# Layer 0 of a hybrid encoder trunk: k norms, low-rank products, logits and inverse roots written another way

## The chip, the cores and the metric

The kernel runs on one core of a Trainium2 chip. The time is that of the device, in microseconds, from the first to the last instruction of the program; lower is better. All arithmetic is in 32 bits. TensorE multiplies numbers of type fp32 in two instructions, and numbers of type fp32r in one; the kernel reaches the accuracy of fp32 with fp32r by splitting an operand into a high part (rounded to fp32r) and a low part (what the rounding left), and by adding the products high x high, high x low and low x high.

## What is computed

The reference has two layers over 1024 positions of width 1024. Layer 0 mixes positions with two groups of heads side by side, layer 1 with chunked attention; each layer then has a squared-ReLU MLP and a gated embedding. Only layer 0 and one helper are touched here. Its parts, cut to what the change names:

```python
# group A (RWKV-7, 8 heads of 64): decay and learning rate from a second low-rank product
w_log = -softplus(-(w0 + tanh(xw @ w1) @ w2)) - 0.5
a = sigmoid(a0 + (xa @ a1) @ a2)
...
# group B (gated DeltaNet, 4 heads of 128)
q = l2norm(heads(qkv[..., :B_WIDTH])) * (B_HEAD_DIM ** -0.5)
k = l2norm(heads(qkv[..., B_WIDTH:2 * B_WIDTH]))
beta = sigmoid(beta_logit)                                       # logits: h @ 8 columns of the input weight
g = -exp(a_log) * softplus(alpha_logit + dt_bias)
o = chunk_gated_delta_rule(q, k, v, beta, g)                     # k_dec = k * exp(gc_last - gc)
o = rmsnorm(o, norm_g) * silu(gate)
```

Here l2norm divides by the root of the sum of squares plus 1e-6, and rmsnorm by the root of the mean square plus 1e-6.

## The kernel before

Activations are kept transposed: 128 partitions hold 128 channels, the free axis holds positions. Layer 0 works on two halves of 512 positions. In each half there are eight units, alternately a pair of RWKV heads and one DeltaNet head: 16 units in all. A unit passes five stages: **in** (dense products of the input with 128 columns of weight at a time), **front** (everything before the triangular inverse), **mid** (the inverse), **back** (the recurrence over four chunks of 128) and **post** (output norm and gate).

Each stage is a generator, and `run` interleaves them as lanes: there is one lane each for in, mid, back and post, two for front, and one for the cumulative decays. A lane that yields a name sleeps for the time that the table `LAT` gives for it, on a clock that only matrix products advance; a lane that yields a tuple waits until another lane has marked it. So the order of the work is made when the program is written out: small products of a lane that is ready go between the dense products, which are last in line. A scheduler that simulates the engines then orders the instructions of each engine, and each engine works through its queue in that order.

The dense product (`dense_part`, `mm3`, all products by the helper `mm` at L180, transposes by `tr` at L195) takes three passes for each of 8 blocks of 128 input channels: high weight with the high and the low part of the input, low weight with the high part. Weights come by DMA on SyncE's queue into a ring `wraw` of two buffers, ScalarE casts the high part (L306), VectorE subtracts the low part (L307). Results are read from PSUM by VectorE.

PSUM in this layer: two banks `dense` for the dense products, two banks `tp` that the front lanes and the post lane share (tiles named `tp`, `st`, `sc`, `pp` in the profile), and single banks for mid and back (`iz`, `pm`, `ch`, `y`). Work tiles of 128x512 come from pools with a number of slots: 11 slots `f` for the fronts and the in lane (`L0_FRONT`), 14 slots `b` for what the fronts hand to back and post (`L0_BACK`). A tile waits until its slot is free.

What the change and the prediction touch:

- `rsqrt_small` (L285 to L294): 1 / sqrt(x) on VectorE for a few numbers per partition. A first guess by integer arithmetic on the bits (L289), then three Newton steps of three operations each (L292 to L294): ten operations, each on the result of the one before. It is called by `row_stats` (sums over all channels), `rwkv_post`, `gdn_front`, `gdn_post` and, in layer 1, `attn_in`.
- `lora`: the first low-rank product, at the start of each half. For decay and learning rate its result is `lwa`, 128x512, in fp32 (tile `lao`); the upper 64 rows get a tanh.
- `rwkv_front`: the second low-rank product, two fp32 products over 64 rows each, `wa2` with `lwa`, put next to each other by `together` (rows of the profile: `tp<-lao,wa`). After it come the tanh and the running sums that give the decay.
- `gdn_logits`: the 8 logit columns as a dense product. A zeroed tile of 128x1024 takes 8 columns of each 128; it is split and multiplied like every other weight, three passes for each of 8 blocks. `gdn_scalars` transposes the 8 rows of the result in 4 pieces and computes beta and the decay.
- `gdn_front`: after the convolutions of k and q (tile `KQ`) come the squares of both on ScalarE (L1081), sums over the 128 channels by one-column products with the squares as stationary operand (rows `st<-ones,f`, 8 fp32 products, 16 instructions), the inverse roots of all 8 columns, and from them `cs`, `ncs`, `hin` (for k) and `phi` (for q). Then the score products in two pairs (`sc<-KQ`), each into a bank `tp`, read with `ncs`. Then the start of the inverse, the convolution of v, and four transposes of k whose result ScalarE scales into `kd` (L1132).
- `gdn_post`: output norm. The sum of squares of the output comes by one-column products; VectorE squares `phi`, combines the two, takes the inverse root and multiplies by `phi` again (L1189 to L1193).
- `masks`: the constants `blk`, `blkr` and `cent`.

Of the kernel before, what the change touches and what calls it, by code (L numbers as in the profile page):

```python
# [8 lines left out]
F32 = mybir.dt.float32  # L9
# [8 lines left out]
P = 128  # L18
# [13 lines left out]
L0_FRONT = {"raw": 6, "f": 11}  # L32
# [80 lines left out]
class Trunk:  # L113
# [140 lines left out]
    def masks(self, cst):  # L254
# [19 lines left out]
        self.blk = cst.tile([P, P], F32, tag="blk", name="blk")  # L274
        nc.gpsimd.memset(self.blk, 0.0)
        nc.gpsimd.memset(self.blk[0:64, 0:64], 1.0)
        nc.gpsimd.memset(self.blk[64:128, 64:128], 1.0)
        self.blkr = cst.tile([P, P], F32R, tag="blkr", name="blkr")
        nc.vector.tensor_copy(self.blkr, self.blk)
        self.cent = cst.tile([P, P], F32, tag="cent", name="cent")  # L280
        nc.gpsimd.tensor_scalar(self.cent, self.blk, -1.0 / 64, None, op0=ALU.mult)
# [3 lines left out]
    def rsqrt_small(self, out, x, shape, tag):  # L285
# [3 lines left out]
        nc.vector.tensor_scalar(out.bitcast(I32), x.bitcast(I32), -0.5, 1597463007.0,  # L289
                                op0=ALU.mult, op1=ALU.add)  # L290
        for _ in range(3):
            nc.vector.tensor_tensor(w, out, out, op=ALU.mult)  # L292
            nc.vector.scalar_tensor_tensor(w, w, -0.5, x, op0=ALU.mult, op1=ALU.mult)
            nc.vector.scalar_tensor_tensor(out, w, 1.5, out, op0=ALU.add, op1=ALU.mult)  # L294
# [275 lines left out]
    def l0_in(self, units):  # L570
# [3 lines left out]
        for u, (nm, p, hf) in enumerate(units):  # L574
            if u % 8 == 0:
# [32 lines left out]
                if hf == 0:  # L608
# [6 lines left out]
                    self.wa2 = fr.tile([P, 512], F32, tag="wa2", name="wa2")  # L615
                    nc.sync.dma_start(out=self.wa2, in_=a["wa2"])
# [15 lines left out]
                sc["lwa"] = yield from self.lora(0, [(0, 64, 0), (64, 128, 1)], "la")  # L632
                nc.scalar.activation(sc["lwa"][0:64], sc["lwa"][0:64], AF.Tanh)
# [56 lines left out]
    def lora(self, i, mus, key, between=None):  # L690
# [16 lines left out]
        out = (self.l0 if key == "lg" else self.fr).tile([P, HB], F32, tag=key + "o", name=key + "o", bufs=2 if key == "lg" else 1)  # L707
# [8 lines left out]
    def gdn_logits(self):  # L716
        nc, a = self.nc, self.a
        raw = self.wp.tile([P, 1024], F32, tag="wraw", name="wraw")
        nc.gpsimd.memset(raw, 0.0)
        nc.sync.dma_start(out=raw.rearrange("p (k c) -> p k c", k=NK)[:, :, 0:8], in_=a["wba"])  # L720
        ba = self.t2()
        yield from self.dense_half(self.split_w(raw), lambda ps: nc.vector.tensor_tensor(ba[0:8, 0:HB], ps[0:8], self.rs[0:8],
                                                                                         op=ALU.mult))
        return ba
# [1461 lines left out]
```

## Time and profile before

| | us |
|---|---|
| median of 3 runs | 3078.52 |
| lowest and highest of them | 3070.69, 3079.13 |
| the profiled execution | 3086.63 |
| its span, first to last instruction of the cores' records | 3084.8 |
| TensorE busy in the span | 2970.1 (96%) |
| VectorE, ScalarE, GpSimd busy | 2209.9, 1486.2, 552.9 |

PE is TensorE's products, PEld its weight loads, DVE VectorE, ACT ScalarE, POOL GpSimd, SP SyncE. A row of the timeline gives the start, the length, the engine, the line, the operation, the tiles (out<-in) with their sizes, how many instructions were merged, and in brackets the idle time before them and what ended it. A row of a group gives the count, the busy time, the mean of one in ns, and the engine's idle time before the group. A wait is "who <- for whom: total us, times, longest". The granted clock is TensorE's, as a share of its full speed. Because products are pipelined, the length of a product is more than the time it holds the queue; that is read from one start to the next.

### The profile page before, as it was taken

The page shows a single profiled execution, that of the slowest core. Times are in us where ns is not written, and L with a number is a line of the kernel's source. Part 1 is how long each engine was busy: PE and PEld are TensorE (multiplying, and loading weights), DVE is VectorE, ACT ScalarE, POOL GpSimd, SP SyncE. Part 2 cuts the span into 40 slices and gives each one's busy share as a digit, 9 for nine tenths or more (in the row PEclk, how much of TensorE's full clock was granted, in tenths as well). Part 3 has the DMA queues.
Part 4 walks back from the last instruction along what each step waited for, and adds up shares of the span by engine and source line. Part 5 has one row for each costly group of instructions (what it writes and reads, how often), then busy time and mean ns, then how long its engine had stood idle before and what let it go on. Part 6 is the DMA issues. An engine that isn't in the chain of part 4 may idle for free.

```text
span 3084.8 us, 47290 instructions
## 1 busy us (share of the span) xinstructions
PE 2970.1 (96%) x17254; PEld 2457.1 (80%) x17254; DVE 2209.9 (72%) x4546; ACT 1486.2 (48%) x2957; POOL 552.9 (18%) x985
## 2 busy tenths in 40 slices
PE   8999999999999999999999999999999999999999
PEld 6777777777777888788887988898878888888887
DVE  7556766667758777788887676676768777788883
ACT  4333433434437555544444465565757555544441
POOL 5434442443500000000005111111210000000002
PEclk9899999999999999999999999999999999999999
DMA  4212112212346444754424211110256444654433
GB/s 145 64 55 62 54 49 75 61 55 68 110 157 227 162 150 151 262 166 151 151 95 131 70 44 40 43 61 23 75 181 223 163 154 153 237 190 150 150 103 116
DMA packets 194857, 368.49 MB, mean 119 GB/s; under 512 B 46800, under 2 KB 49088, under 8 KB 194624
## 3 DMA queue, kind: packets, MB, share of 16 engines
q1 hardware_dynamic: 163808, 309.35, 31.4%
q10 hardware_dynamic: 30816, 56.11, 4.7%
q8 instruction: 136, 2.23, 0.3%
q14 instruction: 97, 0.79, 0.1%
HBM read 268.86 MB, written 96.53 MB: 118 GB/s over the span
## 4 chain that ended last, share of the span: by engine, by line
PE 71%; DVE 14%; DMA 6%; ACT 4%; issue 2%; POOL 1%; SPq 0%; ACTq 0%; DVEq 0%; POOLq 0%
PE dps L180 57%; PE ch L180 2%; PE po L180 2%; DVE act L1283 2%; PE pm L180 1%; PE iz L180 1%; PE pt L195 1%; DMA late<-in_w 1%; PE sn L180 1%; PE tp L180 1%; DMA late<-hd 1%; DVE late L1431 1%; DMA wraw<-in_w_out 1%; PE py L180 1%; DVE wlo L307 1%
## 5 line engine op out<-in xcount | busy, mean ns | idle before, releaser
L180 PE MATMUL dps<-r,act 128*128 128x512 f32 x3720 | 872.9, 392 | 2.0 <-DVE xw L1550 0.8
L180 PEld LDWEIGHTS dps<-r,act 128*128 128x128 f32 x3720 | 698.0, 188 | 157.0 <-issue 1.2
L180 PE MATMUL dps<-xg,whi 128*128 128x512 f32 x1280 | 436.0, 421 | 11.2 <-ACT whi L306 7.4
L1647 POOL TENSOR_TENSOR pn<-pn,prs 128x512 f32<-128x512 f32 x32 | 47.3, 1483 | 1542.6 <-ACT prs L389 1419.5
L180 PE MATMUL dps<-wq,act 128*128 128x384 f32 x1536 | 307.8, 347 | 13.8 <-DVE vs L1909 6.0
L180 PEld LDWEIGHTS dps<-xg,whi 128*128 128x128 f32 x1280 | 236.2, 197 | 62.2 <-ACT whi L306 7.6
L180 PEld LDWEIGHTS dps<-wq,act 128*128 128x128 f32 x1536 | 269.6, 193 | 17.7 <-DVE vs L1909 7.6
L180 PE MATMUL dps<-xg,wlo 128*128 128x512 f32 x640 | 260.7, 407 | 2.6 <-DVE wlo L307 2.6
L1282 ACT CAST act<-act 128x512 fp32r<-128x512 f32 (+2 forms) x281 | 159.3, 600 | 142.0 <-PE dps L180 59.8
L1283 DVE TENSOR_TENSOR act<-act 128x512 fp32r<-128x512 f32 (+2 forms) x281 | 180.1, 669 | 4.6 <-ACT act L1282 4.6
L180 PE MATMUL dps<-act 128*128 128x512 f32 x720 | 176.5, 393 | 2.0 <-DVE late L1404 2.0
L1282 ACT CAST act<-late 128x512 fp32r<-128x512 f32 x210 | 123.7, 620 | 100.4 <-PE dps L180 73.8
L180 PE MATMUL dps<-late,act 128*128 128x512 f32 x672 | 166.6, 392 | 0.0
L180 PEld LDWEIGHTS dps<-act 128*128 128x128 f32 x720 | 136.2, 189 | 32.1 <-DVE late L1404 2.4
L1283 DVE TENSOR_TENSOR act<-late,act 128x512 fp32r<-128x512 f32 x210 | 139.1, 687 | 31.1 <-ACT act L1282 30.9
L180 PEld LDWEIGHTS dps<-xg,wlo 128*128 128x128 f32 x640 | 125.0, 195 | 32.5 <-DVE wlo L307 3.8
L180 PEld LDWEIGHTS dps<-late,act 128*128 128x128 f32 x672 | 126.0, 188 | 27.7
L180 PE MATMUL dps<-xw,act 128*128 128x512 f32 x576 | 145.9, 392 | 0.2 <-ACT act L1282 0.2
L1550 DVE TENSOR_TENSOR xw<-xw,dps 128x512 f32<-128x512 f32 x192 | 130.0, 682 | 17.3 <-PE dps L180 17.2
L306 ACT CAST whi<-wraw 128x1024 fp32r<-128x1024 f32 (+1 forms) x79 | 81.8, 1035 | 107.6 <-PE dps L180 77.1
L180 PEld LDWEIGHTS dps<-xw,act 128*128 128x128 f32 x576 | 107.9, 188 | 24.4 <-ACT act L1282 0.7
L180 PE MATMUL po<-ptile,vs 128*128 128x256 f32 (+1 forms) x576 | 106.8, 295 | 15.5 <-ACT ptile L352 9.7
(488 smaller groups left out, 5600.7 us busy)
## 6 DMA issues: line engine op xcount, KB each, us to landing
hb<-late ACTq DMA_DIRECT2D x196, 256.0 KB
act<-hb SPq DMA_DIRECT2D x158, 256.0 KB
late<-in_w SPq DMA_DIRECT2D x60, 512.0 KB
act<-in_w SPq DMA_DIRECT2D x112, 256.0 KB
wraw<-in_w_in SPq DMA_DIRECT2D x55, 512.0 KB
braw<-hb SPq DMA_DIRECT2D x80, 256.0 KB
wraw<-in_w_out SPq DMA_DIRECT2D x21, 512.0 KB
wraw<-in_w_qkv SPq DMA_DIRECT2D x21, 512.0 KB
```

What stands on the lines that cost most here:

```text
L180: return self.begin(self.nc.tensor.matmul(out, lhsT, rhs, start=start, stop=stop, skip_group_check=again))
L195: return self.begin(self.nc.tensor.transpose(out, in_, ident))
L306: nc.scalar.copy(hi, raw)
L307: nc.vector.tensor_tensor(lo, raw, hi.bitcast(F32), op=ALU.subtract)
L1282: A.copy(hi, s)
L1283: V.tensor_tensor(lo, s, hi.bitcast(F32), op=ALU.subtract)
L1431: V.tensor_tensor(t, u, v, op=ALU.subtract)
L1550: V.tensor_tensor(x[n][:, hs[hf]], x[n][:, hs[hf]], ps, op=ALU.add)
L1647: G.tensor_tensor(pn, pn, prs[:, sl], op=ALU.mult)
```

## The change

In words:

- `rsqrt_small` takes another first guess, one Newton step with tuned constants (three operations) and one step of higher order (four operations): eight in all.
- `wa2` and the first low-rank result `lwa` are split into high and low parts of type fp32r; each of the two second products becomes three fp32r passes instead of one fp32 product. `wa2` is loaded through the ring `wraw`. The unsplit `lwa` is now a work tile `f`.
- `gdn_logits` loads the 64 numbers per partition without a zeroed tile, puts the high and low parts of the 8 columns side by side as 16 columns, and takes two passes for each block (high and low part of the input). `gdn_scalars` transposes 16 rows, and one reduction adds the two halves.
- `gdn_front` makes the four transposes of k before the norms. ScalarE squares each transposed piece straight from PSUM and sums along the row in the same instruction, with the result tile `kd` as scratch; then it scales the pieces into `kd` from the same bank. The inverse root is taken for the 4 columns of k only. The squares of q and their four sums come later, the sums after the convolution of v; `phi` becomes a constant times the sum plus a constant.
- `gdn_post` needs one operation instead of three ahead of its root and none behind it, since q's norm only enters through the epsilon.
- `blk` becomes a view of `blkr`, and the work slots `f` go from 11 to 10.

The diff, cut:

```diff
-L0_FRONT = {"raw": 6, "f": 11}
+L0_FRONT = {"raw": 6, "f": 10}
...
     def rsqrt_small
-        nc.vector.tensor_scalar(out.bitcast(I32), x.bitcast(I32), -0.5, 1597463007.0,
+        nc.vector.tensor_scalar(out.bitcast(I32), x.bitcast(I32), -0.5, 1595932665.0,
                                 op0=ALU.mult, op1=ALU.add)
-        for _ in range(3):
-            nc.vector.tensor_tensor(w, out, out, op=ALU.mult)
-            nc.vector.scalar_tensor_tensor(w, w, -0.5, x, op0=ALU.mult, op1=ALU.mult)
-            nc.vector.scalar_tensor_tensor(out, w, 1.5, out, op0=ALU.add, op1=ALU.mult)
+        d = 0.375 * 0.703952253
+        nc.vector.tensor_tensor(w, out, out, op=ALU.mult)
+        nc.vector.scalar_tensor_tensor(w, w, -d, x, op0=ALU.mult, op1=ALU.mult)
+        nc.vector.scalar_tensor_tensor(out, w, 2.38924456 * d, out, op0=ALU.add, op1=ALU.mult)
+        nc.vector.scalar_tensor_tensor(w, out, 64.0 / 9, out, op0=ALU.mult, op1=ALU.mult)
+        nc.vector.tensor_tensor(w, w, x, op=ALU.mult)
+        nc.vector.scalar_tensor_tensor(w, w, -10.0 / 3, w, op0=ALU.add, op1=ALU.mult)
+        nc.vector.scalar_tensor_tensor(out, w, 5.0, out, op0=ALU.add, op1=ALU.mult)
...
     def l0_in
-                    self.wa2 = fr.tile([P, 512], F32, tag="wa2", name="wa2")
-                    nc.sync.dma_start(out=self.wa2, in_=a["wa2"])
+                    self.wa2 = fr.tile([P, 2, 512], F32R, tag="wa2", name="wa2")
+                    wa2 = self.wp.tile([P, 512], F32, tag="wraw", name="wraw")
+                    nc.sync.dma_start(out=wa2, in_=a["wa2"])
+                    self.split_w(wa2, 512, [self.wa2[:, e] for e in range(2)])
...
-                sc["lwa"] = yield from self.lora(0, [(0, 64, 0), (64, 128, 1)], "la")
-                nc.scalar.activation(sc["lwa"][0:64], sc["lwa"][0:64], AF.Tanh)
+                lwa = yield from self.lora(0, [(0, 64, 0), (64, 128, 1)], "la")
+                nc.scalar.activation(lwa[0:64], lwa[0:64], AF.Tanh)
+                sc["lwa"] = fr.tile([P, 2, HB], F32R, tag="lao", name="lao")
+                self.split_scaled(sc["lwa"], lwa, None, slice(0, HB))
...
     def gdn_logits
-        raw = self.wp.tile([P, 1024], F32, tag="wraw", name="wraw")
-        nc.gpsimd.memset(raw, 0.0)
-        nc.sync.dma_start(out=raw.rearrange("p (k c) -> p k c", k=NK)[:, :, 0:8], in_=a["wba"])
+        raw = self.wp.tile([P, NK, 8], F32, tag="wraw", name="wraw")
+        nc.sync.dma_start(out=raw, in_=self.a["wba"])
+        w = self.wp.tile([P, NK, 16], F32R, tag="whi", name="wba")
+        nc.scalar.copy(w[:, :, 0:8], raw)
+        nc.vector.tensor_tensor(w[:, :, 8:16], raw, w[:, :, 0:8].bitcast(F32), op=ALU.subtract)
+        ba, ps = self.t2(), self.bank()
+        for k in range(NK):
+            for part in range(2):
+                self.mm(ps[0:16], w[:, k, :], self.xg[k][:, part, :], start=k + part == 0, stop=k + part == NK)
+            yield 0
...
     def rwkv_front
-        self.together([self.mm(ps, self.wa2[r, p * P:(p + 1) * P], sc["lwa"][r], start=True, stop=True)
-                       for ps, r in ((psa, slice(64, 128)), (psw, slice(0, 64)))])
+        self.together([self.mm(ps, self.wa2[r, w, p * P:(p + 1) * P], sc["lwa"][r, x], start=w + x == 0, stop=w == 1)
+                       for w, x in ((0, 0), (0, 1), (1, 0)) for ps, r in ((psa, slice(64, 128)), (psw, slice(0, 64)))])
...
     def gdn_front
-        sqs = []
-        for i in range(2):
-            sq = t512()
-            A.activation(sq.rearrange("p (c t) -> p c t", c=4), KQ[:, :, i, :], AF.Square)
-            sqs.append(sq)
         yield "gdn_front1"
-        pst = self.psf.tile([P, HB], F32, tag="tp", name="st")
-        for i in range(2):
-            for c in range(4):
-                self.mm(pst[:, 4 * i + c:4 * i + c + 1], sqs[i][:, c * C:(c + 1) * C], self.ones[:, 0:1],
-                        start=True, stop=True)
-        V.tensor_scalar(ss, pst[:, 0:8], 4e-6, None, op0=ALU.add)
-        self.rsqrt_small(nu, ss, [P, 8], "k")
+        pk = self.psf.tile([P, HB], F32, tag="tp", name="tp")
+        kd = self.t2([P, 4, P], "b")
+        for c in range(4):
+            self.tr(pk[:, c * P:(c + 1) * P], KQ[:, c, 0, :], self.ident)
+        for c in range(4):
+            A.activation(kd[:, c, :], pk[:, c * P:(c + 1) * P], AF.Square, accum_out=ss[:, c:c + 1])
+        for c in range(4):
+            A.activation(kd[:, c, :], pk[:, c * P:(c + 1) * P], AF.Copy, scale=sc["ekd"][:, c, n:n + 1])
+        V.tensor_scalar(ss, ss, 4e-6, None, op0=ALU.add)
+        self.rsqrt_small(nu, ss, [P, 4], "k")
...
+        sq = t512()
+        A.activation(sq.rearrange("p (c t) -> p c t", c=4), KQ[:, :, 1, :], AF.Square)
         for cp in range(2):
             ps = self.psf.tile([P, 2, 2, C], F32, tag="tp", name="sc")
...
         conv(2, vv.rearrange("p (c t) -> p c t", c=4))
-        pk = self.psf.tile([P, HB], F32, tag="tp", name="tp")
-        kd = self.t2([P, 4, P], "b")
+        pst = self.psf.tile([P, HB], F32, tag="tp", name="st")
         for c in range(4):
-            self.tr(pk[:, c * P:(c + 1) * P], KQ[:, c, 0, :], self.ident)
-        for c in range(4):
-            A.activation(kd[:, c, :], pk[:, c * P:(c + 1) * P], AF.Copy, scale=sc["ekd"][:, c, n:n + 1])
+            self.mm(pst[:, c:c + 1], sq[:, c * C:(c + 1) * C], self.ones[:, 0:1], start=True, stop=True)
+        V.tensor_scalar(phi, pst[:, 0:4], 1.28e-4, 5.12e-10, op0=ALU.mult, op1=ALU.add)
...
     def gdn_post
-        V.tensor_tensor(ms, phi, phi, op=ALU.mult)
-        V.scalar_tensor_tensor(ms, pn[:, 0:4], 1.0 / 128, ms, op0=ALU.mult, op1=ALU.mult)
-        V.tensor_scalar(ms, ms, 1e-6, None, op0=ALU.add)
+        V.scalar_tensor_tensor(ms, pn[:, 0:4], 1.0 / 128, phi, op0=ALU.mult, op1=ALU.add)
         self.rsqrt_small(fr, ms, [P, 4], "o")
-        V.tensor_tensor(fr, fr, phi, op=ALU.mult)
```

38 lines of the change are left out of this document (17 added, 21 removed).

## The prediction

> **What bounds the kernel now.** I read the page first, then the busy time by stage, then TensorE's waits in the first stage, then single stretches of the timeline. The first line is the page's; the rest is the view of windows. After the window and its length it gives busy us and count for each engine, then the granted clock.
>
> ```profile
> span 3084.8 us, 47290 instructions
> ```
>
> ```profile
> core 0: us, PE busy (x) PEld busy (x) DVE busy (x) ACT busy (x) POOL busy (x), PEclk, DMA share, GB/s
> 0.00:930.00 930.00, 880.39 (x7086) 679.04 (x7086) 602.08 (x1340) 359.99 (x733) 379.93 (x843) 0.94 0.26 80
> 930.00:1690.00 760.00, 754.79 (x3306) 617.79 (x3303) 593.73 (x927) 384.27 (x667) 43.67 (x27) 1.00 0.50 165
> 1690.00:2260.00 570.00, 517.77 (x3249) 490.60 (x3249) 407.55 (x1288) 345.36 (x865) 107.38 (x100) 0.96 0.17 56
> 2260.00:3085.00 825.00, 817.18 (x3619) 669.63 (x3617) 606.52 (x994) 396.58 (x694) 21.91 (x16) 1.00 0.49 165
> ```
>
> TensorE is busy throughout. Almost everything the diff touches lies in the first window, layer 0 up to its MLP: 880 of 930 us busy, at a granted clock of 0.94. So two things are lost there: some 50 us of idle time, and speed. VectorE is busy 65% and ScalarE 39% of that window. The next view says who ends TensorE's idle time in it (total, times, longest):
>
> ```profile
> PE pm L180 <- DVE PMQ L942: 9.8, 5, 3.4
> PE dps L180 <- ACT whi L306: 7.4, 1, 7.4
> ...
> PE dps L195 <- DVE cc L865: 3.4, 1, 3.4
> ```
>
> No wait repeats for every head group; the stage is not paced by one engine behind TensorE. It is one queue of dense passes with chains of small products mixed in. There, a pass taken off TensorE is time off the stage, unless what replaces it makes the queue stand.
>
> **The change part by part.** *Logits.* A dense pass in a clean stretch:
>
> ```profile
> 307.16 0.62 PE L180 MATMUL dps<-xg,whi 128*128 128x512 f32 x2
> 307.63 0.40 PE L180 MATMUL dps<-xg,wlo 128*128 128x512 f32 x1
> 307.86 0.62 PE L180 MATMUL dps<-xg,whi 128*128 128x512 f32 x2
> ...
> 308.54 0.62 PE L180 MATMUL dps<-xg,whi 128*128 128x512 f32 x2
> ```
>
> Six passes start in 1.38 us: 0.23 each. The logits took three passes for each of 8 row blocks in both halves of the sequence; now two, with the high and low part of the 8 weight columns side by side. 2 x 8 x 0.23 = **3.7 us** less. The zeroing of a 128x1024 tile on GpSimd, the wide cast and the wide subtraction go too, all beside dense work. The final transposes are as many as before, with 16 rows instead of 8.
>
> *Norms of q and k.* In fp32, each one-column product is two instructions:
>
> ```profile
> 117.81 1.95 PE L180 MATMUL st<-ones,f 128*128 128x1 f32 x16
> 119.62 0.48 PE L180 MATMUL dps<-xg,wlo 128*128 128x512 f32 x1
> ```
>
> ```profile
> L180 PE MATMUL st<-ones,f 128*128 128x1 f32 x128 | 15.7, 247 | 0.6 <-ACT f L1081 0.6
> ```
>
> Sixteen hold the queue for 119.62 - 117.81 = 1.81 us. The k half goes, the q half moves behind the convolution of v. Half of 1.81, in 8 head groups: **7.2 us** less. The four transposes of k existed already and only move forward, so they cost nothing new.
>
> *Second low-rank product.* Two fp32 products per head group, over rows 64 to 127 and 0 to 63, two passes each, become three fp32r passes each:
>
> ```profile
> 46.81 1.12 PE L180 MATMUL tp<-lao,wa 64*128 64x512 f32 x2
> 47.87 0.73 PE L180 MATMUL dps<-xg,whi 128*128 128x512 f32 x2
> 48.53 1.12 PE L180 MATMUL tp<-lao,wa 64*128 64x512 f32 x2
> 49.58 0.50 PE L180 MATMUL dps<-xg,wlo 128*128 128x512 f32 x1
> ```
>
> Two fp32 passes take 1.06 us, 0.53 each; 32 of them, one after the other, 17.0 us. New: 48 passes at the dense 0.23 are 11.0 us. But they alternate between the two halves of the rows. Do halves run side by side? Sixteen alternating 64-row passes of 128 columns, beside full-array passes of 256 columns:
>
> ```profile
> 68.60 1.16 PE L180 MATMUL tp<-AR,b 64*128 64x128 f32 x16
> 69.60 0.82 PE L180 MATMUL pm<-AR,b 64*128 64x128 f32 x4
> ```
>
> ```profile
> 820.42 1.02 PE L180 MATMUL sc<-KQ 128*128 128x256 f32 x4
> 821.28 0.55 PE L180 MATMUL ch<-b,PMQ 128*128 128x64 f32 x4
> ```
>
> 0.063 us each, against 0.86 / 4 / 2 = 0.108 per 128 columns on the full array: halves do overlap. So the new cost is 5.5 us (all paired) to 11.0, the old 8.5 to 17.0. The ends are a loss of 2.5 and a gain of 11.5; I take serial against serial, **6.0 us**, because the row at 46.81 shows the old halves apart.
> The Trainium skill's "TensorE: Matmul & The Clock Gate" (Part 3, Packing small matmuls) says that products in different row groups run concurrently; the row at 68.60 agrees, and by that rule alone the new passes would cost 5.5 us.
>
> TensorE in all: 3.7 + 7.2 + 6.0 = **16.9 us less**.
>
> *VectorE.* The small operations of the inverse root:
>
> ```profile
> 420.54 0.17 DVE L289 TENSOR_SCALAR fr<-mso 128x4 int32<-128x4 int32 x1
> 420.74 0.16 DVE L292 TENSOR_TENSOR rsw<-fr 128x4 f32<-128x4 f32 x1
> ...
> 422.51 0.16 DVE L1193 TENSOR_TENSOR fr<-fr,phi 128x4 f32<-128x4 f32 x1
> ```
>
> A dependent step costs 0.20 us, and its engine 0.16. Two fewer per root, in 27 roots of this stage, and three fewer in each of 8 output norms: 78 x 0.16 = 12.5 us of busy time. A norm's chain becomes 0.4 to 1.0 us shorter. I count nothing: TensorE has dense passes during these chains. Without that cover it would be at most 8 x 1.0 for the output norms, gained. New are three 512-wide subtractions (two low-rank results, one weight):
>
> ```profile
> L307 DVE TENSOR_TENSOR wlo<-wraw,whi 128x512 fp32r<-128x512 f32 x2 | 1.4, 723 | 0.3 <-ACT whi L306 0.3
> ```
>
> 3 x 0.72 = 2.2 us. The one behind each low-rank result stands, with its cast, ahead of a half's first decay products: 2 x some 1.3 us later, beside the dense passes around 46.81. Likewise the 16 roots in attention lose 32 steps of VectorE, which there is not TensorE's bound; nothing counted.
>
> *ScalarE and the bank.* One square of 512 per head group goes; four squares of 128 that also sum come, ahead of the four scaled copies that read the same PSUM bank:
>
> ```profile
> L1081 ACT ACTIVATE f<-KQ x16: 612/622/634, 113.8 to 814.4; 128x512 f32<-128x512 f32 x16
> ```
>
> ```profile
> 131.15 1.14 ACT L1132 ACTIVATE b<-tp,gs_ekd 128x128 f32<-128x128 f32 x4 [2.05 <-PE tp L195]
> ```
>
> ```profile
> L2037 ACT ACTIVATION_READ_ACCUMULATOR pb<-pb,mx 128x1 f32 x128 | 24.6, 192 | 0.0
> ...
> L1132 ACT ACTIVATE b<-tp,gs_ekd 128x128 f32<-128x128 f32 x32 | 9.1, 369 | 9.3 <-PE tp L195 9.3
> ```
>
> No square of this form is in the trace. By the copy and attention's read of a sum it is 0.37 + 0.19 = 0.56 us, four of them 2.25; pipelined as the copies are, 1.14 + 4 x 0.19 = 1.9. ScalarE gains some 13 us of work at 39% load. What matters is the bank, one of two that the front and post lanes share: held for about 0.5 + 2.25 + 1.14 = 3.9 us, where the one-column sums held theirs 1.95 + 0.16 = 2.1. Queued behind a wait for it on TensorE: the second pair of score products and every dense pass after them; on ScalarE, behind squares that wait for transposes, the casts of the next weights. Bounds: 0 (the scores wait for the root anyway) to 8 x 1.8 = 14 us; I take 2, since the scores' results cannot be read before the root.
>
> *Start, slots.* The weight of the low-rank product now goes through the two-buffer ring of the weights, ahead of the low-rank loads on SyncE's queue. From nothing to one turn of the ring, 2 x 0.72 us of cast and subtraction plus the load, some 4 us; I take 1. The work slots drop from 11 to 10, but the gdn front no longer holds both squares: nothing counted, and a rival.
>
> Sum: -16.9 + 2 + 1 = -14 us. Against the profiled execution's 3086.63 us that is 3072.6. This execution lies 8.1 us above the median of the three runs, 3078.52, so the same difference gives **3064.5**.
>
> **The rivals.** *The bank cancels it.* The second score pair is queued before the copies end, in every gdn head group: -16.9 + 14 + 1 = -2, **3077**. For it: only two banks. Against it: the scores' own evacuation waits for the same squares and root.
>
> *The time comes back as idle.* The 50 us of idle time say that parts of the stage are paced by chains. If only a third of the passes saved was on the path, 16.9 / 3 = 5.6 remains: **3073**. Against it: 95% busy. It is also the case in which the change removes the passes, as it says, and TensorE waits instead.
>
> *Slower: the tenth slot.* A front operation on ScalarE waits for a work slot, with the weights' casts queued behind it; dense passes starve, and the clock falls. What one such stand costs, from a stand that the trace has:
>
> ```profile
> 59.19 0.56 PE L195 MATMUL dps<-ident,f 8*128 8x8 f32 x4 [3.40 <-DVE cc L865]
> 59.85 1.19 PE L180 MATMUL dps<-xg,whi 128*128 128x512 f32 x2
> ...
> 61.27 1.05 PE L180 MATMUL dps<-xg,whi 128*128 128x512 f32 x2
> ```
>
> ```profile
> 59.20:66.00 6.80, 6.70 (x19) 5.28 (x20) 6.78 (x12) 0.84 (x2) 5.93 (x4) 0.50 0.23 77
> ```
>
> 3.4 us idle, and then 6.8 us at half the clock (three passes in 1.42 us instead of 0.69), which loses another 3.4: 6.8 us in all. Three such stands (16.9 / 6.8 = 2.5) eat the gain; five make 34 - 14 = +20, **3098**. For it: fourteen slots could be wanted when both fronts are at their fullest. Against it: fronts run two units ahead, and a gdn front frees slots earlier.
>
> *More than that.* The low-rank halves pair (11.5 instead of 6.0), and the clock falls less often. After the sixteen one-column products it fell, with TensorE busy all the time:
>
> ```profile
> 117.00:120.60 3.60, 3.60 (x33) 3.06 (x32) 3.56 (x7) 2.29 (x3) 1.67 (x2) 1.00 0.05 17
> 120.60:124.00 3.40, 3.40 (x10) 2.66 (x9) 3.19 (x10) 1.35 (x2) 1.45 (x2) 0.51 0.51 154
> ```
>
> 3.4 us at 0.51 lose 1.7 us; two of those gone is 3.4 more. -14 - 5.5 - 3.4 = -23: **3055.5**. The Trainium skill's "TensorE: Matmul & The Clock Gate" (Part 1) explains the halved clock by a monitor of the array's activity over windows of about 3.4 us; the 3.4 us stretch here agrees.
>
> **How the numbers follow.** The forecast gets 0.45, with a range of its own of 3058 to 3071 (0.05 of it above the bound for faster); the larger gain 0.13; the bank 0.13 and the idle 0.12; the slower case 0.17. About 0.3%, 9.2 us, is what a measurement of this kernel can tell from no change: faster is below 3069.3, slower above 3087.8. Faster 0.40 + 0.13 = 0.53; same 0.05 + 0.13 + 0.12 = 0.30; slower 0.17. The range runs from 3050 (both halves paired and some clock) to 3088, and leaves out the slower case and little else.
>
> **What would show it.** In the profile after: 32 passes of the logits instead of 48, 64 instead of 128 one-column sums of q and k, 48 low-rank passes near 0.23 us or half that; busy time of TensorE in layer 0 lower by about 17 us, idle time not higher, clock not below 0.94. Layer 0 ends some 14 us earlier and the three later windows keep their lengths. Wrong would be: waits of the scores for ScalarE's copies (the bank), dense passes waiting for casts (the slot), or a layer 0 with less busy time and the same end.

## The result and the profile after

The changed kernel takes 3060.42 us (median of 8 runs, 3057.44 to 3068.92); the kernel before, run beside it, 3073.6 (8 runs, 3068.79 to 3080.96). The ratio is 0.9954, with an interval of 0.9941 to 0.9968: some 13 us, or 0.46%, faster. The forecast of 3064.5 us, 14 us below the time before, holds as a number. Where the time came from is another matter, and by what follows the agreement is luck.

The page, and the four windows of the prediction, now for the changed kernel:

```profile
span 3058.4 us, 47093 instructions
```

```profile
0.00:930.00 930.00, 874.10 (x7059) 674.60 (x7060) 592.05 (x1276) 369.22 (x802) 380.50 (x841) 0.94 0.26 83
930.00:1690.00 760.00, 751.21 (x3295) 615.59 (x3294) 593.50 (x920) 380.75 (x662) 50.96 (x33) 1.00 0.50 164
1690.00:2260.00 570.00, 526.67 (x3351) 497.34 (x3351) 417.02 (x1301) 358.98 (x894) 97.86 (x94) 0.98 0.19 64
2260.00:3058.00 798.00, 792.85 (x3491) 649.58 (x3489) 585.84 (x936) 377.67 (x658) 21.63 (x16) 1.00 0.49 163
```

Fixed windows cut through different work in the two kernels. Stages are better cut at events. The second product of each MLP reads `r` and `act`, so its first and last start mark the MLPs; what lies before the first is layer 0, what lies between the two MLPs is attention. The view of lines gives after the mean and its neighbours the first and last start; before's two rows, then after's:

```profile
L180 PE MATMUL dps<-r,act x1716: 388/392/501, 972.3 to 1626.9; 128*128 128x512 f32 x191
...
L180 PE MATMUL dps<-r,act x2004: 388/392/503, 2368.4 to 3079.1; 128*128 128x512 f32 x183
```

```profile
L180 PE MATMUL dps<-r,act x1716: 388/392/502, 962.3 to 1615.8; 128*128 128x512 f32 x191
...
L180 PE MATMUL dps<-r,act x2004: 388/392/477, 2343.9 to 3052.7; 128*128 128x512 f32 x183
```

So layer 0 went from 972.3 to 962.3 us (-10.0), the first MLP from 654.6 to 653.5, **attention from 741.5 to 728.1 (-13.4)**, the rest from 716.4 to 714.5. The prediction had counted nothing for attention. The view of windows for layer 0 and attention, before and then after (length; busy us of TensorE, its loads, VectorE, ScalarE, GpSimd; granted clock):

```profile
0.00:972.30 972.30, 920.66 (x7256) 710.76 (x7257) 638.89 (x1395) 389.66 (x782) 379.93 (x843) 0.95 0.28 88
1626.90:2368.40 741.50, 687.97 (x4037) 631.66 (x4036) 528.50 (x1464) 435.12 (x1015) 143.55 (x122) 0.97 0.26 85
```

```profile
0.00:962.30 962.30, 905.13 (x7192) 699.53 (x7193) 621.09 (x1320) 392.54 (x841) 380.50 (x841) 0.95 0.28 89
1615.80:2343.90 728.10, 679.67 (x4037) 624.10 (x4036) 526.83 (x1430) 435.16 (x1016) 141.03 (x122) 0.98 0.26 87
```

In attention TensorE issues exactly the same 4037 products, and only VectorE has fewer operations (1464 to 1430; 32 of them are the steps that 16 roots lost). Yet TensorE's idle time fell by 741.50 - 687.97 - (728.10 - 679.67) = 5.1 us, and its clock rose from 0.97 to 0.98. Summed from the trace's record of the clock, it ran at about half for 47.8 us before and 30.7 after. An interval at half clock does half the work, so that is worth some 17.1 / 2 = 8.6 us (an estimate). 5.1 + 8.6 = 13.7, against 13.4 measured.

A warning goes with the two profiles: their spans differ by 26.4 us, the medians by 13. Before's profiled execution took 3086.63 us, 13 more than the median of its kernel here. Experiments below had to show how much of the -10.0 in layer 0 is chance.

### The profile page after: what moved, and what is told of

Its sections match the earlier page's. It is cut to its first block, busy times and chain, and to the rows that moved or that the text cites. A ratio compares the mean times of both kernels' runs of the same rounds, so it can differ in the third digit from the quotient of the medians.

```text
span 3058.4 us, 47093 instructions
## 1 busy us (share of the span) xinstructions
PE 2944.8 (96%) x17190; PEld 2437.1 (80%) x17190; DVE 2188.4 (72%) x4431; ACT 1486.6 (49%) x3016; POOL 550.9 (18%) x983
## 4 chain that ended last, share of the span: by engine, by line
PE 76%; DVE 11%; DMA 5%; ACT 4%; issue 2%; POOL 2%; SPq 0%; ACTq 0%; DVEq 0%; POOLq 0%
PE dps L180 62%; PE ch L180 2%; PE po L180 2%; PE pt L195 1%; PE pm L180 1%; PE iz L180 1%; PE sn L180 1%; PE tp L180 1%; DVE act L1291 1%; DMA wraw<-in_w_qkv 1%; DMA late<-hd 1%; DMA late<-in_w 1%; DVE f L1083 1%; PE py L180 1%; PE pp L180 1%
## 5 line engine op out<-in xcount | busy, mean ns | idle before, releaser
L180 PE MATMUL dps<-xg,whi 128*128 128x512 f32 x1248 | 423.6, 420 | 13.5 <-ACT whi L311 9.3
L1558 DVE TENSOR_TENSOR xw<-xw,dps 128x512 f32<-128x512 f32 x192 | 130.2, 682 | 16.3 <-PE dps L180 15.9
```

Source lines behind the costliest of these rows:

```text
L180: return self.begin(self.nc.tensor.matmul(out, lhsT, rhs, start=start, stop=stop, skip_group_check=again))
L1558: V.tensor_tensor(x[n][:, hs[hf]], x[n][:, hs[hf]], ps, op=ALU.add)
```

## The experiments

My first theory was the prediction's, **passes**: the time goes with the passes taken off TensorE in layer 0, so the parts act one by one and add up. Against it stood **chains** (the shorter roots on VectorE are what counts) and **order** (each edit makes the scheduler order all the engines anew, and the time follows that order). The four parts were put alone into the kernel before.

`e_logits`: only the logits with 16 columns and two passes.

```diff
-        yield from self.dense_half(self.split_w(raw), lambda ps: ...)
+        for k in range(NK):
+            for part in range(2):
+                self.mm(ps[0:16], w[:, k, :], self.xg[k][:, part, :], start=k + part == 0, stop=k + part == NK)
```

> The kernel before with the logits alone as in the change: 32 passes for them instead of 48. The theory of the passes (what leaves TensorE's queue in layer 0 leaves the time): 16 x 0.23 = 3.7 us faster. The theory of the chains (the time comes from shorter chains of small VectorE operations): no change, within 1 us. The theory of the order (any change that makes the scheduler write another order moves the time by some 10 us, whatever it saves): anything between -10 and +10 us, not near -3.7.

`e_norms`: only `gdn_front` and `gdn_post` of the change, with roots of ten operations.

```diff
-            A.activation(sq.rearrange("p (c t) -> p c t", c=4), KQ[:, :, i, :], AF.Square)
+            A.activation(kd[:, c, :], pk[:, c * P:(c + 1) * P], AF.Square, accum_out=ss[:, c:c + 1])
```

> The kernel before with the DeltaNet front and output norm alone as in the change, the inverse roots still of ten operations: 64 one-column instructions fewer. Theory of the passes: 7.2 us less TensorE time, less up to 2 us for the longer hold of the bank: 5 to 7 us faster. Theory of the chains: 3 us faster at most (three VectorE operations fewer in each of 8 output norms, 0.6 us each, were all of it on the path 4.8). Theory of the order: anything within 10 us either way.

`e_lora`: only the second low-rank product in fp32r parts, with its ring load, the ten slots and the shared `blk`.

```diff
-        self.together([self.mm(ps, self.wa2[r, p * P:(p + 1) * P], sc["lwa"][r], start=True, stop=True)
+        self.together([self.mm(ps, self.wa2[r, w, p * P:(p + 1) * P], sc["lwa"][r, x], start=w + x == 0, stop=w == 1)
```

> The kernel before with the second low-rank product alone as in the change (fp32r parts, the weight through the ring, ten work slots, the shared constant): 48 fp32r passes instead of 32 fp32 passes. Theory of the passes: 17.0 us of queue become 10 (the changed kernel's trace shows most passes side by side with their partner), so 6 us faster, less 1 for the start. Theory of the chains: slower by 1 to 3 us, since a cast and a subtraction of 0.7 us each come ahead of the products in both halves. Theory of the order: anything within 10 us.

`e_roots`: only `rsqrt_small` with eight operations, in both layers.

```diff
-        for _ in range(3):
...
+        nc.vector.scalar_tensor_tensor(w, w, -10.0 / 3, w, op0=ALU.add, op1=ALU.mult)
+        nc.vector.scalar_tensor_tensor(out, w, 5.0, out, op0=ALU.add, op1=ALU.mult)
```

> The kernel before with the inverse roots of eight operations alone. No TensorE pass changes. Theory of the passes: no change, within 2 us. Theory of the chains: 8 to 13 us faster, most of it in the attention layer, which is 13 us shorter in the changed kernel's profile than in the one before. Theory of the order: anything within 10 us.

Measured against 3073.64 us of the kernel before (28 runs); layer 0 and attention are read from one profile each, cut as above. The profiled execution of `e_logits` is the slowest of its twelve, 13 us above their median, so its two stages read too long:

| | median us | ratio, 95% | layer 0 | attention |
|---|---|---|---|---|
| e_logits | 3066.33 | 0.9972, 0.9957 to 0.9987 | 972.1 | 738.6 |
| e_norms | 3053.66 | 0.9927, 0.9904 to 0.9950 | 953.1 | 731.6 |
| e_lora | 3069.08 | 0.9976, 0.9962 to 0.9991 | 963.6 | 738.1 |
| e_roots | 3061.38 | 0.9956, 0.9941 to 0.9972 | 962.9 | 727.2 |

Every part alone makes the kernel faster: -7.3, -20.0, -4.6 and -12.3 us by medians. The sum is -44; together they give -13. Passes alone does not stand. The low-rank product came out near the passes' -5, the roots in the chains' range; the logits gave more than passes or chains allow, and the norms' -20.0 lies outside all three expectations. The norms alone beat the whole change, and the roots, counted at nothing, are worth as much as all of it.

The next four asked whether the roots and the norms lie in separate places of the program, or whether order makes the parts disagree.

`e_old_roots`: the changed kernel with roots of ten operations everywhere.

```diff
-        d = 0.375 * 0.703952253
...
+        for _ in range(3):
```

> The changed kernel with the inverse roots of ten operations put back. Alone, the four parts measured -7, -20, -5 and -12 us by the medians, 44 together, and the whole change only -13; so at least one part loses something beside the others. The theory that the roots act in the attention layer, where no other part does anything, and so add to whatever layer 0 does: about 12 us slower than the changed kernel, no faster than the kernel before (within 4 us of it). The theory that the parts only roll another order in layer 0: anything between 10 us faster and 10 us slower than the changed kernel.

`e_norms_roots`: `e_norms` with the roots of eight operations too.

```diff
-        for _ in range(3):
...
+        nc.vector.scalar_tensor_tensor(out, w, 5.0, out, op0=ALU.add, op1=ALU.mult)
```

> The kernel before with the DeltaNet norms and the new roots, without the low-rank product and the logits. Theory of separate places (norms in layer 0, roots mostly in attention): -20 and -12 add to some 30 us faster than the kernel before, about 3043 us, and faster than the changed kernel by 17. Theory of a rolled order: the gain of the norms alone was a lucky order, so it does not carry over: near the changed kernel, 3055 to 3065 us.

`e_ten_slots`: the kernel before with ten slots `f`.

```diff
-L0_FRONT = {"raw": 6, "f": 11}
+L0_FRONT = {"raw": 6, "f": 10}
```

> The kernel before with ten work slots instead of eleven, nothing else: no instruction more or less, only another order where a slot is late. Theory of the passes and chains: no change (within 2 us), or a few us slower where fronts wait for a slot. Theory of the order: a move of 5 us or more, either way, without any work saved.

`e_scalars_late`: the changed kernel with the small products of `gdn_scalars` behind the second dense product of `lora`, away from its start, where TensorE stands.

```diff
+        sb = yield from self.project(wb, key, 1)
         if between is not None:
...
-        sb = yield from self.project(wb, key, 1)
```

> The changed kernel with the transposes of the logits (and all of gdn_scalars) put behind the second product of the gate's low-rank pair instead of the first, 24 dense passes or 5.5 us later in TensorE's queue. In the changed kernel's profile TensorE stands 4.9 us there, for VectorE's copy of the logits, and then runs at half the clock for 10.2 us. The theory that this stand is lost time: 5 to 10 us faster than the changed kernel. The rival that the DeltaNet front, which needs the decays, is what sets the pace there: no change, or slower by up to 5 us.

Measured against 3075.55 us (25 runs):

| | median us | ratio, 95% | layer 0 | attention |
|---|---|---|---|---|
| e_old_roots | 3082.09 | 1.0023, 1.0007 to 1.0040 | 972.4 | 741.2 |
| e_norms_roots | 3068.71 | 0.9991, 0.9976 to 1.0005 | 973.2 | 725.4 |
| e_ten_slots | 3073.88 | 1.0001, 0.9986 to 1.0016 | 967.3 | 741.0 |
| e_scalars_late | 3058.24 | 0.9956, 0.9940 to 0.9971 | 965.1 | 721.6 |

Without the short roots the change is 6.5 us slower than before and 22 slower than with them, where some 12 had been expected. With norms and short roots together, 13 us of the norms' 20 are gone, and the 3068.71 us lie above the ranges of both theories: attention is at 725.4, but layer 0, whose fronts differ from those in `e_norms` by the shorter roots alone, went from 953.1 to 973.2. `e_scalars_late` did nothing for layer 0 (965.1 against 962.3), as its rival said. That does not settle what the stand at the start costs: TensorE still waits 2.09 us for the same copy, instead of 4.92.

`e_ten_slots` turned out the most useful for another reason: its instructions stand in the same order as before's on every engine, so no tile ever waits for the eleventh slot, and the run is a repeat of before. Its windows, to be held against before's above:

```profile
0.00:967.30 967.30, 911.45 (x7256) 704.28 (x7257) 637.17 (x1396) 390.72 (x782) 381.17 (x843) 0.96 0.28 88
1619.80:2360.80 741.00, 688.60 (x4037) 632.12 (x4036) 528.84 (x1462) 434.80 (x1013) 143.15 (x122) 0.97 0.26 85
```

One order of instructions, and layer 0 takes 972.3 or 967.3 us; attention repeats to 0.5 us here, but `e_lora`, which has TensorE's order of before in attention, took 738.1 there. A difference of 5 us in one profile's layer 0, or of 3 to 4 in its attention, says nothing.

So the stages had to be changed one at a time, with the order in the other stage held. The roots of attention have a tag of their own in the code, "q". The theory now: attention's roots bring the whole gain, and layer 0's parts cancel among themselves. Its rival: layer 0 brings it. For the mechanism I supposed that VectorE's queue in attention is what counts, with a price for each operation; a root of thirteen should then cost as a root of eight saves.

`e_q8_only`: the kernel before, with eight operations for tag "q" only. `e_norms_q8`: the same edit in `e_norms`.

```diff
-        nc.vector.tensor_scalar(out.bitcast(I32), x.bitcast(I32), -0.5, 1597463007.0,
+        if tag == "q":
+            nc.vector.tensor_scalar(out.bitcast(I32), x.bitcast(I32), -0.5, 1595932665.0,
...
+        else:
```

> The kernel before with the eight-operation root in the attention layer alone (16 calls); layer 0 keeps its ten operations and its order of TensorE's instructions. So far the attention layer took 731.6 to 741.5 us in six profiles with ten operations and 721.6 to 728.1 in four with eight, though the trace shows the roots' result lying 2 us and more before its use. Theory that the whole change's 13 us come from there (VectorE's queue in attention, and the clock that falls after TensorE's stands): 11 to 15 us faster than the kernel before, attention 722 to 729 us, layer 0 unchanged. Rival, that layer 0 brings the gain as the prediction had it, and the shorter attention in the profiles is chance: within 3 us of the kernel before.

> The DeltaNet norms of the change in layer 0 with roots of ten operations there (alone 20 us faster than the kernel before), and the eight-operation root in attention alone. The two stages are apart: layer 0 keeps the order that it had with the norms alone. Theory of separate stages: 953 us for layer 0 again and attention 722 to 729 instead of 731.6, so 3 to 10 us faster than with the norms alone, 3044 to 3051 us, the fastest so far. Rival, that gains do not add anywhere (as norms and roots together were slower than either): 3055 us or more.

`e_q10_changed`: the changed kernel, with ten operations for tag "q" only.

```diff
+        if tag == "q":
...
+            for _ in range(3):
```

> The changed kernel with ten operations put back in the attention layer alone; layer 0 is the changed one, in its order of TensorE's instructions. Theory that attention brings the gain: 11 to 15 us slower than the changed kernel, no different from the kernel before (within 3 us), attention 731 to 742 us. Rival, that layer 0 brings it: within 3 us of the changed kernel, some 13 us faster than before.

`e_q13_before`: the kernel before, with a fourth Newton step for tag "q".

```diff
+        if tag == "q":
...
+            for _ in range(4):
```

> The kernel before with a fourth Newton step in the attention layer's roots alone: 13 operations instead of 10 in 16 calls, 48 more. Theory of VectorE's queue (each of these operations delays what is behind it, and TensorE's stands grow with them): slower than the kernel before by 10 to 20 us, attention 750 us or more. Rival, that only the order of the attention layer was rolled and eight operations happened on a good one: no direction, within 10 us either way.

Measured against 3073.74 us (23 runs). The profiled execution of `e_q8_only` lies 4.5 us below its median, that of `e_ten_slots` above lies 6 over its own:

| | median us | ratio, 95% | layer 0 | attention |
|---|---|---|---|---|
| e_q8_only | 3056.68 | 0.9941, 0.9924 to 0.9959 | 964.0 | 718.6 |
| e_norms_q8 | 3048.58 | 0.9913, 0.9896 to 0.9929 | 950.5 | 727.2 |
| e_q10_changed | 3073.23 | 0.9997, 0.9987 to 1.0008 | 967.1 | 737.6 |
| e_q13_before | 3081.43 | 1.0016, 1.0005 to 1.0027 | 968.0 | 741.3 |

Windows of layer 0 and attention in `e_q8_only`, then in `e_q10_changed`, and attention in `e_q13_before`:

```profile
0.00:964.00 964.00, 909.72 (x7257) 702.59 (x7258) 637.17 (x1396) 389.51 (x782) 381.00 (x843) 0.96 0.28 89
1617.70:2336.30 718.60, 674.79 (x4037) 618.65 (x4036) 527.71 (x1434) 435.64 (x1016) 141.09 (x122) 0.99 0.27 88
```

```profile
0.00:967.10 967.10, 910.90 (x7193) 703.57 (x7194) 623.17 (x1320) 393.14 (x841) 381.28 (x841) 0.94 0.28 88
1619.50:2357.10 737.60, 682.11 (x4036) 625.82 (x4035) 531.44 (x1461) 435.28 (x1016) 142.19 (x122) 0.97 0.26 85
```

```profile
1621.80:2363.10 741.30, 686.43 (x4036) 630.23 (x4035) 538.61 (x1512) 433.71 (x1014) 141.72 (x122) 0.97 0.26 85
```

`e_q8_only` and `e_q10_changed` settle where the gain is. Two operations fewer in the 16 roots of attention, alone, give -17.1 us, more than the 11 to 15 expected. Everything else of the change, alone, gives -0.5 (interval -4 to +2.5). The two do not add up to the -13 of the whole, but come within 5 us of it. Nor is each part of everything else without effect: `e_old_roots`, with ten operations in layer 0 too, is some 8 us slower than `e_q10_changed` by the ratios, whose intervals just touch. TensorE's order in layer 0 is before's in the first and the changed kernel's in the second, so layer 0 itself can be read twice over: with before's order it took 972.3, 967.3, 964.0 and 968.0 us (mean 967.9), with the changed order 962.3 and 967.1 (mean 964.7). By these profiles the change is worth some 3 us there, less than the spread of one order; it is not worth 10 or 14.

The expectation of `e_q13_before` missed. It costs 7.7 us by medians and some 5 by the ratio (1.5 to 8), not 10 to 20: the direction that the queue's theory gave, the size that the rival allowed. Its attention in the profile, 741.3, is no longer than before's, but before's two profiles lie 13 and 6 us above the median of their kernel and this one 2 below its own. 48 operations more cost 5 us, 32 fewer bring 17: one price for each operation doesn't fit both.

`e_norms_q8` came out as expected: 25.2 us faster than before and 12 faster than the change. It is the best version found. Its windows:

```profile
0.00:950.50 950.50, 903.59 (x7193) 696.19 (x7194) 629.88 (x1371) 393.31 (x838) 384.49 (x843) 0.96 0.28 90
1603.30:2330.50 727.20, 679.09 (x4036) 623.85 (x4035) 520.71 (x1430) 433.44 (x1013) 140.97 (x122) 0.98 0.26 87
```

It leaves the logits, the low-rank product and layer 0's own roots as they were, and its layer 0 has the order of `e_norms`: 950.5 and 953.1, the only layer 0 clearly below 960.

## Why the prediction was right in its number and wrong in its place

**The step that failed** is the sentence "Likewise the 16 roots in attention lose 32 steps of VectorE, which there is not TensorE's bound; nothing counted." By the experiments these steps are worth 17 us in the kernel before and 13 in the changed one, which is the whole gain. On `e_norms` they brought only 5, within the noise; its attention had come out shorter, 731.6, without any edit there. In seven profiles with ten operations attention takes 731.6 to 741.5 us, in six with eight operations 718.6 to 728.1, without overlap. That VectorE isn't the bound by its busy share (71%) was true, and not a reason. What ends TensorE's idle time there repeats: before's waits in attention (total, times, longest) come eleven times from the copy of a score tile (`ptile`), five times from `vs`, and so on; below them the same three in `e_q8_only`:

```profile
PE po L180 <- ACT ptile L352: 9.7, 11, 1.8
PE dps L180 <- DVE vs L1909: 6.0, 5, 2.8
...
PE pt L195 <- ACT pb L2034: 4.2, 4, 1.5
```

```profile
PE po L180 <- ACT ptile L365: 8.2, 10, 1.6
...
PE dps L180 <- DVE vs L1922: 4.4, 5, 1.8
...
PE pt L195 <- ACT pb L2047: 2.0, 2, 1.1
```

I had read the waits of layer 0 only. A stage that isn't touched by name still deserves its own list of waits, if an operation in it gets shorter.

How two operations come to that much is seen in part. A stretch of attention before, as windows and as rows of the timeline:

```profile
1871.70:1875.10 3.40, 3.06 (x24) 2.81 (x22) 3.15 (x14) 1.21 (x4) 2.13 (x1) 1.00 0.47 154
1875.10:1878.50 3.40, 2.09 (x14) 1.39 (x12) 1.73 (x9) 2.28 (x9) 0.00 (x0) 1.00 0.00 0
1878.50:1881.90 3.40, 2.98 (x13) 2.62 (x13) 3.02 (x10) 1.08 (x3) 0.00 (x0) 0.50 0.00 0
```

```profile
1872.81 1.07 PE L180 MATMUL po<-ptile,vs 128*128 128x256 f32 x7
...
1876.83 0.55 PE L195 MATMUL pt<-ident,pb 128*128 128x128 f32 x3 [0.75 <-ACT pb L2034]
...
1878.78 0.58 PE L180 MATMUL po<-ptile,vs 128*128 128x256 f32 x1 [0.80 <-ACT ptile L352]
...
1879.84 1.84 PE L180 MATMUL po<-ptile,vs 128*128 128x256 f32 x7
```

In the interval from 1875.10 TensorE stands in one wait of 0.75 us and in most of another of 0.80, with small gaps besides; it is busy for 2.09 of 3.40 us, and the next 3.4 us run at 0.50: seven products that took 1.07 us in the first row take 1.84 in the last. This one is a mild case: in before's attention 9 intervals have 1.5 us or more of idle time, and 14 run at half clock; in `e_q8_only` 3 and 4. Idle time there went from 53.5 to 43.8 us, time at half clock from 47.8 to 13.7. Waits of half a microsecond or more number 39 before and 32 in `e_q8_only`, 44.3 and 34.5 us in all, so fewer intervals have the idle time after which the clock falls.

What is **open** is why the shorter root makes these waits fewer. By the trace the time from the root's start to the multiplication that uses it falls from 4.74 to 3.84 us on average, but before and after the change its result lies unused for at least 1.7 us before the transposes that read it, so TensorE doesn't wait for the root itself. Either VectorE's other work moves forward behind it, or the scheduler, which counts with shorter operations, writes a better order for TensorE. That order is another one in attention whenever the root there changes, and also in `e_logits` and `e_norms`, which touch nothing there. The seven profiles with ten operations hold five different orders, the six with eight hold five others, so one lucky order isn't the whole answer. `e_q13_before` speaks against a simple price for each operation on the queue. Holding the order while changing the number of operations was not tried.

**The passes.** They went, as predicted. The groups of the changed kernel in the first 930 us, and two of the eight low-rank products:

```profile
L180 PE MATMUL tp<-lao,wa 64*128 64x512 f32 x48 | 11.1, 441 | 0.0
...
L180 PE MATMUL st<-ones,f 128*128 128x1 f32 x64 | 8.7, 257 | 1.7 <-DVE b L1132 1.7
...
L180 PE MATMUL dps<-xg,wba 128*16 128x512 f32 x32 | 8.2, 394 | 0.0
```

```profile
122.83 0.49 PE L180 MATMUL tp<-lao,wa 64*128 64x512 f32 x1
123.26 0.43 PE L180 MATMUL iz<-T,N 32*32 32x16 f32 x30
123.62 0.96 PE L180 MATMUL tp<-lao,wa 64*128 64x512 f32 x5
124.51 0.29 PE L180 MATMUL iz<-T,N 32*32 32x16 f32 x10
```

```profile
418.15 0.97 PE L180 MATMUL tp<-lao,wa 64*128 64x512 f32 x6
419.06 1.33 PE L180 MATMUL dps<-xg,wba 128*16 128x512 f32 x5
```

48, 64 and 32, as counted. The six low-rank passes of the second group hold the queue for 419.06 - 418.15 = 0.91 us: at 0.23 each, one after the other, they would take 1.38. In the trace the two halves of a pair start 3 to 4 ns apart. But only two of the eight groups go in one piece. In the others the first pass goes alone, as at 122.83, for 0.43 us, and the other five take 0.89: 1.32 us, and 1.5 in the group at 213. That makes 9.9 us for the 48. The old products took at most 15.9: 2 x 1.06 in seven groups, and 1.06 in the one at 336.00, where the halves went side by side. The saving is then some 6 us. It is the prediction's 6.0 by another sum: that took old and new passes one after the other at 0.53 and 0.23, while the new ones go in pairs of some 0.30 or alone for 0.43, so that the size came out right partly by luck.

TensorE's work in layer 0 can be estimated as its length less idle time less half of the time at half clock: 870.4 us (mean of four profiles) became 851.7 (two), -18.7. Counting at half clock only the time in which TensorE was busy, it is -15.8. The predicted -16.9 lies between.

**What was given back.** Of these 16 to 19 us layer 0 kept some 3. So the sentence on it, "a pass taken off TensorE is time off the stage, unless what replaces it makes the queue stand", left out the clock. Idle time rose from 54.0 to 56.7 us, and the time at half clock from 87.0 to 112.7, which loses some 10 to 13 by the two estimates; intervals with 1.5 us or more of idle time number 9 to 13 in the four profiles with before's order, 13 and 15 in the two with the changed one. So the rival "the time comes back as idle" is what layer 0 did, with a fifth or a sixth of the saving kept instead of a third, and mostly as a lower clock. The stage's granted clock in the first profile of each kernel, 0.95 in both, didn't show it: it takes means over several. The waits that I could name at the start of the changed kernel (timeline):

```profile
54.49 1.05 PE L180 MATMUL tp<-hsel,f 128*128 128x2 f32 x8 [3.17 <-ACT f L851]
...
60.46 0.61 PE L195 MATMUL dps<-ident,f 16*128 16x16 f32 x4 [4.92 <-DVE f L738]
```

look like the culprits. In `e_scalars_late` the first is gone and the second is 2.09 us; new waits of 0.87 and 1.35 us came, and the clock still fell there, for 6.83 us instead of 10.24. Layer 0 was no shorter, so what these stands cost stays open. That the loss depends on the order as well as on the parts is what `e_norms` (953.1) and `e_norms_roots` (973.2) suggest: the same fronts but for shorter roots, TensorE in another order, 20 us apart, while the short roots alone left layer 0 no longer (962.9 in `e_roots`). Which stands of the new order make the difference is open.

**Roots and norms in layer 0** were counted at -7.2 for the products and nothing for the chains. The norms alone gave -20.0, of which some 16 in layer 0 (951.8, mean of two, against 967.9), about a third each from passes, idle time and clock by the first estimate. The passes' share, 6 to 7 us, is close to the 7.2 predicted; for the idle time and the clock that go with them the prediction had no term.

**The bank** was priced at 2 us, its rival at 14. Next to nothing of it is there. ScalarE's squares, timeline of the changed kernel:

```profile
109.22 0.28 ACT L1100 ACTIVATE b<-tp 128x128 f32<-128x128 f32 x1 [1.28 <-PE tp L195]
109.39 0.20 ACT L1100 ACTIVATION_READ_ACCUMULATOR b<-tp 128x1 f32 x1
...
110.23 0.39 ACT L1102 ACTIVATE b<-tp,gs_ekd 128x128 f32<-128x128 f32 x1
```

Four squares with their sums take 110.23 - 109.22 = 1.01 us, not 1.9 to 2.25: a square and the read of its sum overlap with the next. The waits of TensorE in the first 930 us of the changed kernel have no score product that waits for the copies; the one wait for the reading of scores is the 1.7 us of the sums of squares (`st`) in the groups above:

```profile
PE dps L180 <- ACT whi L311: 9.3, 3, 7.0
PE tp L180 <- DVE b L890: 5.7, 3, 2.3
PE dps L195 <- DVE f L738: 4.9, 1, 4.9
PE tp L180 <- ACT f L851: 3.2, 1, 3.2
...
PE sc L180 <- DVE KQ L1087: 0.2, 1, 0.2
```

**The tenth slot**, the rival on the slower side, is not there in the kernel before: with ten slots no instruction changes its place. The changed kernel was not run with eleven; its waits for casts, 9.3 us in all with 7.0 of them in one at the start, are hardly more than before's 7.4. **Start and weight ring** at 1 us can't be told from the spread of layer 0.

**The later stages** did not keep their lengths: the two MLPs did within 2 us, attention did not. That test was the right one to write down, and it is the one that failed.

## What to carry to other kernels

Where a scheduler orders the queues, an edit's own cost is only part of its effect: compare single parts, hold the order of the other stages, and repeat one order to learn its spread, before a few microseconds are given to a cause. Where TensorE is nearly always busy, count the short waits of each stage and how closely they lie, not the busy share of the engine behind them: a shorter chain of tiny operations can pay there more than passes taken away. And try the parts of a change alone and in pairs: here one part and the attention's share of another beat all four by 12 us.

## What the runs showed of the hardware

The clock falls by intervals. Its record has stretches at half clock of 3.41 us or a multiple of it, such as 6.83 and 10.24. In attention, over 14 profiles and cut in steps of 3.41 us along this record, an interval at full clock was followed by one at half in 1 of 2297 cases where TensorE had been idle in it for less than 0.5 us, in none of 285 at 0.5 to 1.0, 24 of 162 at 1.0 to 1.5, 43 of 63 at 1.5 to 2.0, and 29 of 29 at 2.0 or more. So what brings the clock down there isn't the idle time of the whole stage, but, in most cases, some 1.5 us or more of it in one interval, even in several pieces. The Trainium skill's "TensorE: Matmul & The Clock Gate" (Part 1, The HAM clock gate) describes a free-running window of 3413 ns, and these traces agree in its length. The rule that it gives there, no idle gap beyond some 3.4 us, is too lenient for them: in the stretch shown gaps of 0.75 and 0.80 us, 1.31 us of idle time in one interval, were enough.

In layer 0 the same count gives another picture: 43 of 182 falls, about a quarter, come after an interval with less than 0.5 us of idle time, as after the one-column products that the prediction shows. One order of instructions gave 75 to 106 us at half clock in layer 0 in four profiles; the shortest, 964.0 us, has the least and the longest, 972.3, the most. Half of that difference would be 15 us, more than the 8 measured, so half is an upper estimate of what time at half clock costs.
